# Gate vectors by way of DRAM on GpSimd's queue, and weights, chunks and transposed activations in chosen halves of 128-byte lines

## The chip, the cores and the metric

One Trainium2 chip; the kernel runs on one of its cores. The metric is the device time of one execution in microseconds (us). The run shown is one profiled execution; the times are those of three others.

## What is computed

Two blocks on 256 tokens of width 1024, in float32. The first has two layers with a context of 256 tokens beside x; every layer takes six modulation vectors (shift, scale and gate, twice) from silu(c) times a matrix. The second has four layers of other mixers. Cut to what matters here:

```python
for i in range(2):                                   # first block
    m_lat = silu(c) @ ada_w[i] + ada_b[i]            # for x; m_ctx from c_ctx for the context y
    sh1, sc1, g1, sh2, sc2, g2 = split(m_lat, 6)
    h, hc = rms(x, norm1_g[i]) * (1 + sc1) + sh1, rms(y, norm1_g[i]) * (1 + csc1) + csh1
    o, oc = mixer(h, hc)                             # layer 0: Fourier and window attention; layer 1: neighbourhood
    x = x + g1 * o
    x = x + g2 * swiglu(rms(x, norm2_g[i]) * (1 + sc2) + sh2)
    if i == 0:                                       # the same for the context, with cg1 and cg2
        y = y + cg1 * oc
        y = y + cg2 * swiglu(rms(y, norm2_g[i]) * (1 + csc2) + csh2)
for i in range(4):                                   # second block: retention, convolution, dilated attention, retention
    x = x + rms(mixer(rms(x, w[i, 0])), w[i, 1])
    x = x + rms(swiglu(rms(x, w[i, 2])), w[i, 3])
```

## The kernel before

A product in float32 is made of three fast passes: each operand is split into a high and a low part (`whi` and `wlo` for weights, `hTh` and `hTl` for transposed activations, `ckh` and `ckl` for chunks), and `mm3` (line 484) adds high x high, high x low and low x high. In the profile a matmul stands as out<-moving,stationary.

Weights come in blocks of 1 MB (128 partitions x 2048 float32) on SyncE's queue into one of three raw tiles (`Weights.load`, line 246). ScalarE makes the high part and VectorE the low part, by halves (`Weights.split`, line 280), into a slot: "0" to "2" always, "3" and "4" in some stages. Slot "3" is the place of the context's transposed activations, the second half (e = 1) of the tiles `hTh` and `hTl`; slot "4" is a pool of its own behind the fixed pools.

A first product takes 48 matmuls of 256 columns a block: `mm_nat` (line 495) with hT as weights of TensorE and the block streaming, `mm_trans` (line 504) the other way round. A second product, `mm_down` (line 515), takes 24 matmuls of 512 columns a block, 12 for each of two token tiles, with a chunk (the transposed result of the first product) as weights of TensorE and the block streaming; its accumulators are called acc. In the FFN of layer 0 x and the context share a pass: `FfnPair.emit` streams x's hT and the context's hT, 2 x 256 columns, in one matmul. In the even mixer and in the convolution hT itself is reused to hold the chunks.

`Kernel.open` (line 330) makes the pools in this order, one behind the other in every partition: const (consts, small, half), raw (three raw tiles of 8192 bytes), hl (the slots "0" to "2", six tiles of 8192), x (`hTh` and `hTl`, 16,384 bytes each, then x's two tiles), st (small statistics, 1344 bytes), s4, nb. A tile takes a multiple of 32 bytes, and the first one starts on a 128-byte line. Behind nb each stage opens its own pools, slot "4" and the chunks among them; the pools h1 and ada grow from the other end. Retention's pools start with tiles of which one is 32 bytes long, Odd's with one of 256 and one of 32.

The modulation's rows are added up in a tile `rows` of 128 partitions x 512, one for each layer and group g (`ada_unit`, line 2093): output 512 j + n of x stands in partition 32 j, of the context in 32 j + 1. There are eight units k for each group; they run between other work, those of layer 1 within layer 0's FFN and layer 1's mixer. `gate` (line 2139) spreads one gate vector over all partitions: two DMAs on ScalarE's queue, each from one partition of `rows` into half of the tile `gate`, which takes the place of a tile in nb. It is called six times: twice at the end of the even mixer, twice in the middle of layer 0's FFN (after block 5), once in Odd after the second group of heads, once in layer 1's FFN. `gated` (line 2150) multiplies the accumulators by it and adds them to x.

Each engine runs its instructions in the order in which they are written down, and a DMA that it issues stands in that order too. `Pace` estimates when each engine comes to what has been written so far, DMAs counted; put-off stages and splits of weights are placed by it. GpSimd (POOL) computes the powers `ny` of the norms and adds masks to Odd's biases; its queue loads the norm gains of the second block (`gain`, line 389).

Of the kernel before, what the change touches and what calls it, by code (L numbers as in the profile page):

```python
# [7 lines left out]
F32 = mybir.dt.float32  # L8
# [6 lines left out]
D = 1024  # L15
# [9 lines left out]
HOLD = 1200                # no split where a stage is due within this time ...  # L25
HOLD_AHEAD = 1             # ... unless fewer blocks than this are split ahead

# columns of the packed small inputs
# [9 lines left out]
# columns of the packed constants  # L38
CP = {}
_o = 0  # L40
for _n, _w in (("ident", 128), ("rev", 128), ("sel", 256), ("e2", 8), ("diag", 32)):
    CP[_n] = (_o, _w)
    _o += _w
# [3 lines left out]
HALVES = slice(0, 512), slice(512, 1024)  # L47


class Engine:  # L50
    """Passes an engine's instructions on and keeps the pace's account of them."""
# [14 lines left out]
class Pace:  # L66
    """An estimate of when each engine comes to the instructions emitted so far, from the waits that
    the data needs and the price of each instruction. It only steers the order of emission."""

    LAG = {"pe": 190, "act": 40, "dve": 190, "pool": 190}       # from an engine's end to another's start  # L70
    OWN = {"pe": 0, "act": 190, "dve": 125, "pool": 125}        # ... to its own next instruction
# [12 lines left out]
    def entry(self, ap):  # L84
        """Times of the last write, of its engine, and of the last use, by element of the tile."""
# [25 lines left out]
    def ready(self, *aps):  # L111
        """When the data of these is there for another engine."""
        return max(float(self.view(x, self.entry(x)[0]).max()) + self.LAG.get(self.entry(x)[2], 0) for x in aps)

    def free(self, tag, bufs, n):
        """When the next n tiles of this tag are free."""
        hist = next((v for k, v in self.tags.items() if k and k.startswith(tag)), [])
        return max([float(self.tiles[x][1].max()) for x in hist[-bufs:][:n]], default=0.0) if len(hist) >= bufs else 0.0

    def loaded(self, tile):  # L120
        """A block of weights goes into this tile."""
# [45 lines left out]
    def clock(self, start, end):  # L167
        """The tensor engine runs at half its clock after a window in which it was mostly idle."""
# [36 lines left out]
class Weights:  # L205
    """Streams weight blocks: DRAM -> raw -> (high part, low part), ahead of their use.

    Blocks are split, by halves, where the pace has them landed and the engines that split them idle,
    so that no engine waits on a transfer with other work behind it."""

    def __init__(self, K):
# [4 lines left out]
        self.at = -1             # the last block asked for  # L216
        self.part = None         # the block of which one half is split
# [4 lines left out]
        self.slots = []          # free slots, the longest free first  # L222
# [11 lines left out]
    def close_slot(self, name):  # L234
        """No block goes into this slot any more."""
# [43 lines left out]
    def split(self, u):  # L279
        """The next half of block u."""  # L280
# [45 lines left out]
class Kernel:  # L326
# [3 lines left out]
    def open(self, ex):  # L330
# [10 lines left out]
        self.hT = [self.x_p.tile([128, 2, KD, 256], F32R, name=n) for n in ("hTh", "hTl")]  # L341
        self.W = Weights(self)
        self.tasks, self.attns, self.tagged = [], [], {}
        self.mm_n, self.held = 0, []         # tiles "mm" taken so far; those that put-off stages read: [number, task]
# [3 lines left out]
        self.half = self.const_p.tile([128, 8], F32, name="half")  # L348
        self.nc.gpsimd.memset(self.half, -0.5)
        self.nc.scalar.dma_start(out=self.small, in_=self.a["small"])  # L350
        self.nc.scalar.dma_start(out=self.consts, in_=self.a["c_pack"])

# [4 lines left out]
    def open_ext(self, n):  # L357
        """Room for one more weight block ahead; "3" is the place of the context's h^T."""
# [25 lines left out]
    def post(self, gain, bias=None):  # L384
        """x += rms(acc (+ bias)) * gain, in stages."""
# [31 lines left out]
    def block2(self, bin_):  # L417
        """bin_: the boundary before the first sublayer, its A of both tiles done."""
# [10 lines left out]
    def table(self, func):  # L429
        """Have the scalar engine fetch this function's table ahead of its use."""  # L430
# [13 lines left out]
    def rsqrt(self, ss, n, scale, eps, pool, tag="n", bufs=None):  # L444
        """1/sqrt(ss * scale + eps)."""
# [6 lines left out]
    def square(self, ss, src, b):  # L452
        """ss[:, b] = sum of the squares / D of src, half b of [tok, D]."""
# [4 lines left out]
    def rstd(self, ss):  # L458
        """1/sqrt(ss[:, 0] + ss[:, 1] + eps)."""
# [9 lines left out]
    def split_psum(self, hi, lo, ps, act=True):  # L469
        """hi + lo = ps exactly, each with the bits one fast pass carries."""  # L470
# [4 lines left out]
    def bcast_row(self, row, n):  # L475
        """DMA source: a DRAM row of n elements for every partition."""
        return bass.AP(row.tensor, row.offset, [[0, 128], [1, n]])

# [7 lines left out]
    def mm32(self, out, lhsT, rhs, start, stop, share=1, **k):  # L486
        """A float32 product; share: how many run side by side."""
# [7 lines left out]
    def mm_nat(self, key, hT, t, out, parity=False):  # L495
        """out[tok, 256] = h[tok tile t, or the tokens of parity t] @ w block (K = 1024)."""
# [7 lines left out]
    def mm_trans(self, key, hT, out, need=1):  # L504
        """out[feat, j, tok] = (h @ w block)^T for its two 128-feature tiles."""
# [26 lines left out]
    def room(self, tag, n):  # L532
        """Run put-off tasks of this tag until fewer than n are left."""
# [6 lines left out]
    def defer(self, f, src, need=1, tag=None):  # L540
        """Run f (which takes `need` PSUM tiles) once the tensor engine has come to where src is there."""
# [7 lines left out]
    def stage(self, f, src, eng, tag=None, after=None):  # L549
        """Emit f, work of the engine eng, once that engine need not wait for src and `after` holds."""  # L550
# [1819 lines left out]
```

## Time and profile before

| | us |
|---|---|
| median of three runs | 2721.39 |
| lowest and highest | 2714.77, 2721.40 |
| profiled execution: its span, first to last instruction | 2716.9 |

The profiled execution has no time of its own beside its span; the median of the runs lies 4.5 us above that span. The page gives busy times of the engines, the chain of work that ended last, groups of instructions and the DMA issues. A busy time of TensorE (PE) counts overlapping matmuls once; how fast they follow each other is read from their starts in the timeline. PEclk is the granted clock as a share of full speed.

### The profile page before, as it was taken

To read this page: it belongs to the slowest core of one execution; us is meant where nothing else is said; L and a number is where in the kernel's file an instruction comes from. 1 tells how busy PE (TensorE), PEld (TensorE's weight loads), DVE (VectorE), ACT (ScalarE), POOL (GpSimd) and SP (SyncE) were. 2 spreads that over 40 slices of the span, in tenths; PEclk is the share of its full clock that TensorE was granted. 3 is DMA by queue.
4 is the path that set the end of the run, shared out by engine and by line. 5 is a ranking of instruction groups with operands and counts; after the bars stand their busy time and mean duration, and the time that the engine had idled before them with its cause. 6 is when DMAs were issued, how large, how long until landed. Compare 5 with 4: busy or idle time off the path is not lost.

```text
span 2716.9 us, 43849 instructions
## 1 busy us (share of the span) xinstructions
PE 2599.4 (96%) x18444; PEld 2308.7 (85%) x18444; DVE 1496.4 (55%) x2420; ACT 1202.4 (44%) x2050; POOL 108.5 (4%) x156
## 2 busy tenths in 40 slices
PE   6988997999989999999999979999999999999998
PEld 5646875788867999999999869989998999999997
DVE  4475332346647745765645555456555654765643
ACT  4454221235535544544544434445554544544532
POOL 1100000000311000000000000000000000000000
PEclk9998998999989999999999999999999999999999
DMA  7368257545464675564655736545443654564652
GB/s 259 123 215 153 102 185 125 189 155 184 119 129 137 202 176 181 181 199 142 206 182 168 226 89 212 192 140 175 136 132 118 210 186 155 181 202 140 205 186 82
DMA packets 321414, 453.68 MB, mean 167 GB/s; under 512 B 20689, under 2 KB 280913, under 8 KB 316097
## 3 DMA queue, kind: packets, MB, share of 16 engines
q1 hardware_dynamic: 315552, 434.63, 48.1%
q10 hardware_dynamic: 2592, 5.33, 3.7%
q0 software_dynamic: 3072, 10.91, 1.1%
q8 instruction: 145, 2.38, 0.4%
q14 instruction: 53, 0.43, 0.0%
HBM read 445.47 MB, written 2.23 MB: 165 GB/s over the span
## 4 chain that ended last, share of the span: by engine, by line
PE 83%; DVE 6%; DMA 6%; ACT 2%; issue 1%; ACTq 0%; POOL 0%; SPq 0%; DVEq 0%; POOLq 0%
PE mm L60 62%; PE acc L60 21%; DVE wlo L60 2%; DMA wraw<-ev_w_out 1%; DMA wraw<-ada_w 1%; DMA wraw<-ffn_w_up 1%; DVE sm L60 1%; DVE hTl L60 1%; ACT whi L60 1%; DMA u<-up 1%; DMA wraw<-ffn_w_down 1%; ACTq L60 0%; DMA taps<-u 0%; POOL ny L60 0%; DVE hn L60 0%
## 5 line engine op out<-in xcount | busy, mean ns | idle before, releaser
L60 DVE TENSOR_TENSOR wlo<-wraw,whi 128x1024 fp32r<-128x1024 f32 x592 | 701.3, 1225 | 454.4 <-ACT whi L60 453.5
L60 ACT CAST whi<-wraw 128x1024 fp32r<-128x1024 f32 x592 | 592.4, 1048 | 392.7 <-issue 155.7
L60 PE MATMUL mm<-hTh,whi 128*128 128x256 f32 (+1 forms) x1840 | 553.5, 301 | 17.0 <-ACT whi L60 15.2
L60 PE MATMUL mm<-hTh,wlo 128*128 128x256 f32 (+1 forms) x1840 | 552.0, 300 | 0.6 <-DVE wlo L60 0.5
L60 PE MATMUL mm<-hTl,whi 128*128 128x256 f32 (+1 forms) x1840 | 551.9, 300 | 0.3 <-DVE hTl L60 0.3
L60 PE MATMUL mm<-whi,hTh 128*128 128x256 f32 x1616 | 467.8, 290 | 4.1 <-ACT hTh L60 3.2
L60 PE MATMUL mm<-whi,hTl 128*128 128x256 f32 x1616 | 458.7, 284 | 5.5 <-DVE hTl L60 5.5
L60 PE MATMUL mm<-wlo,hTh 128*128 128x256 f32 x1616 | 457.9, 283 | 0.0
L60 PEld LDWEIGHTS mm<-hTh,whi 128*128 128x128 f32 x1840 | 352.7, 192 | 32.0 <-ACT whi L60 16.0
L60 PEld LDWEIGHTS mm<-hTl,whi 128*128 128x128 f32 x1840 | 351.7, 191 | 13.5 <-DVE hTl L60 0.5
L60 PEld LDWEIGHTS mm<-hTh,wlo 128*128 128x128 f32 x1840 | 351.6, 191 | 13.0 <-DVE wlo L60 1.7
L60 PEld LDWEIGHTS mm<-whi,hTh 128*128 128x128 f32 x1616 | 310.4, 192 | 22.7 <-issue 9.7
L60 PEld LDWEIGHTS mm<-whi,hTl 128*128 128x128 f32 x1616 | 310.4, 192 | 7.6 <-DVE hTl L60 7.6
L60 PEld LDWEIGHTS mm<-wlo,hTh 128*128 128x128 f32 x1616 | 310.9, 192 | 0.6
L60 PE MATMUL acc<-whi,ckh 128*128 128x512 f32 x664 | 264.7, 399 | 0.0
L60 PE MATMUL acc<-whi,ckl 128*128 128x512 f32 x664 | 262.6, 395 | 0.6 <-DVE ckl L60 0.6
L60 PE MATMUL acc<-wlo,ckh 128*128 128x512 f32 x664 | 262.6, 395 | 0.4 <-DVE wlo L60 0.4
L60 PE MATMUL mm<-hTh 128*128 128x256 f32 x656 | 188.3, 287 | 0.5 <-ACT hTh L60 0.5
L60 PE MATMUL mm<-hTh,hTl 128*128 128x256 f32 x656 | 186.7, 285 | 0.4 <-DVE hTl L60 0.4
L60 PE MATMUL mm<-hTl,hTh 128*128 128x256 f32 x656 | 186.4, 284 | 0.0
L60 DVE TENSOR_TENSOR hTl<-wraw,hTh 128x1024 fp32r<-128x1024 f32 x116 | 138.9, 1223 | 59.0 <-ACT hTh L60 58.9
L60 DVE TENSOR_TENSOR sg<-sg,mm 128x512 f32<-128x512 f32 (+1 forms) x67 | 40.2, 600 | 228.2 <-PE mm L60 228.2
(245 smaller groups left out, 3335.2 us busy)
## 6 DMA issues: line engine op xcount, KB each, us to landing
wraw<-ffn_w_in SPq DMA_DIRECT2D x88, 1024.0 KB, 5.1
wraw<-ret_w_in SPq DMA_DIRECT2D x48, 1024.0 KB, 5.2
wraw<-ffn_w_out SPq DMA_DIRECT2D x44, 1024.0 KB, 4.9
wraw<-ada_w SPq DMA_DIRECT2D x40, 1024.0 KB, 5.2
wraw<-attn_w_in SPq DMA_DIRECT2D x36, 1024.0 KB, 5.0
wraw<-ffn_w_down SPq DMA_DIRECT2D x33, 1024.0 KB, 4.9
wraw<-ffn_w_gate SPq DMA_DIRECT2D x22, 1024.0 KB, 5.2
wraw<-ffn_w_up SPq DMA_DIRECT2D x22, 1024.0 KB, 5.3
```

What stands on the lines that cost most here:

```text
L60: r = f(*args, **kw)
```

## The change

Three things. The constants lose two tables that nothing reads (sel, e2; 264 columns). Pads and a stride of 64 bytes within `hTh` and `hTl` move tiles: x's hT starts a 128-byte line, the context's hT and slot "3" start at its middle, and everything behind the pool x moves by 704 bytes, in Retention and Odd by 96 less. And `gate` no longer reads `rows` itself: when a group g > 0 is complete, `save_rows` writes the four rows of x (in layer 0 of the context too) to DRAM, and `gate` reads 1024 elements from there for every partition, in one DMA; both are on GpSimd's queue. The two pads of 96 bytes below are Retention's and Odd's. The rest of the diff takes out comments and the entries of the two tables.

```diff
-for _n, _w in (("ident", 128), ("rev", 128), ("sel", 256), ("e2", 8), ("diag", 32)):
+for _n, _w in (("ident", 128), ("rev", 128), ("diag", 32)):
...
+HT_E = KD * 256 + 16
...
-        self.hT = [self.x_p.tile([128, 2, KD, 256], F32R, name=n) for n in ("hTh", "hTl")]
+        self.pad(self.x_p, 64)
+        self.hT = [self.x_p.tile([128, 2 * HT_E], F32R, name=n).rearrange("p (e c) -> p e c", e=2)[:, :, 0:KD * 256]
+                   .rearrange("p e (k c) -> p e k c", k=KD) for n in ("hTh", "hTl")]
...
+        self.pad(self.const_p, 32)
...
+    @staticmethod
+    def pad(pool, n, name="pad"):
+        pool.tile([128, n // 4], F32, name=name)
...
         K.ck_p = pool("ck", 4)
+        K.pad(p1, 96)
...
         K.ck_p = pool("ck", 2)
+        K.pad(p1, 96)
...
         nc.vector.tensor_tensor(out=t, in0=t, in1=ps, op=ALU.add)
+        if k == KD - 1 and g:
+            self.save_rows(l, g)
...
     def gate(self, l, n, e):
         nc = self.nc
         g, x = (1, 0) if n == "g1" else (2, 1)
-        rows = self.rows[l, g]
+        src = self.saved[l, g, e]
         t = self.nb_p.tile([128, D], F32, tag=("gpost", "gpre")[e], name="gate")
-        for h in range(2):
-            r = 32 * (2 * x + h) + e
-            nc.scalar.dma_start(out=t[:, h * 512:h * 512 + 512], in_=rows[r:r + 1, :].rearrange("p (a n) -> p a n", a=1).to_broadcast([1, 128, 512]))
+        nc.gpsimd.dma_start(out=t, in_=self.bcast_row(src[2 * x:2 * x + 2, :], D))
...
+    def save_rows(self, l, g):
+        for e in range(1 if l else 2):
+            self.saved[l, g, e] = d = self.rows_p.tile([4, 512], F32, name=f"rows{l}{g}{e}")
+            self.nc.gpsimd.dma_start(out=d, in_=self.rows[l, g][e:e + 97:32, :])
...
+        K.rows_p = ex.enter_context(tc.tile_pool(name="saved", bufs=1, space=bass.MemoryType.DRAM))
```

## Rows read from the trace of the kernel before

**Rows 1.** The page: busy times by engine, and the chain's shares by engine.
```profile
PE 2599.4 (96%) x18444; PEld 2308.7 (85%) x18444; DVE 1496.4 (55%) x2420; ACT 1202.4 (44%) x2050; POOL 108.5 (4%) x156
...
PE 83%; DVE 6%; DMA 6%; ACT 2%; issue 1%; ACTq 0%; POOL 0%; SPq 0%; DVEq 0%; POOLq 0%
```

**Rows 2.** Stretches: length, busy us (instructions) by engine, granted clock, DMA share, GB/s.
```profile
900.00:1110.00 210.00, 207.74 (x1486) 195.08 (x1487) 120.28 (x136) 98.49 (x133) 3.68 (x6) 1.00 0.67 199
1110.00:1300.00 190.00, 190.00 (x1341) 177.99 (x1341) 120.09 (x168) 93.42 (x145) 5.49 (x10) 1.00 0.48 160
```

**Rows 3.** Timeline of TensorE: start, duration, instruction; the first matmuls of runs.
```profile
944.41 0.28 PE L60 MATMUL mm<-hTh,whi 128*128 128x256 f32 x1
...
950.06 0.40 PE L60 MATMUL acc<-hTh,ckh 128*128 128x512 f32 x1
...
972.77 0.28 PE L60 MATMUL mm<-hTh,whi 128*128 128x256 f32 x1
...
978.21 0.28 PE L60 MATMUL mm<-hTh 128*128 128x256 f32 x1
...
983.97 0.40 PE L60 MATMUL acc<-whi,ckh 128*128 128x512 f32 x1
...
989.58 0.28 PE L60 MATMUL mm<-hTh,whi 128*128 128x256 f32 x1
...
1001.07 0.39 PE L60 MATMUL acc<-whi,ckh 128*128 128x512 f32 x1
...
1006.55 0.28 PE L60 MATMUL mm<-hTh 128*128 128x256 f32 x1
```

**Rows 4.** DMA issues: out<-in, queue, count, KB each, median us to landing.
```profile
gpre<-norm_w POOLq DMA_DIRECT2D x8, 512.0 KB, 5.7
...
gate<-rows ACTq DMA_DIRECT2D x12, 256.0 KB, 21.4
```

**Rows 5.** Stretches while gates are in flight; columns as in group 2.
```profile
222.00:236.00 14.00, 14.00 (x66) 11.65 (x65) 11.24 (x19) 6.11 (x12) 0.57 (x1) 0.99 0.91 34
...
985.00:1010.00 25.00, 25.00 (x170) 23.12 (x169) 9.16 (x9) 7.70 (x9) 0.00 (x0) 1.00 0.93 107
```

**Rows 6.** The chain of waits in order of time: start, length, what.
```profile
203.95 12.45 ACTq L60
...
219.96 22.15 DMA wraw<-ev_w_out
...
404.32 21.79 PE mm L60 x96
...
430.42 20.94 DMA wraw<-ffn_w_up
...
483.29 23.44 PE mm L60 x110
...
512.52 23.63 PE mm L60 x112
```

**Rows 7.** Groups of matmuls by form: count, busy us, mean ns, idle before.
```profile
L60 PE MATMUL mm<-whi,hTh 128*128 128x256 f32 x1616 | 467.8, 290 | 4.1 <-ACT hTh L60 3.2 <-ACT qT L60 0.8
...
L60 PE MATMUL acc<-whi,ckh 128*128 128x512 f32 x664 | 264.7, 399 | 0.0
...
L60 PE MATMUL mm<-hTh,whi 128*128 128x512 f32 x288 | 113.5, 394 | 15.2 <-ACT whi L60 15.2
```

**Rows 8.** Timeline of GpSimd around the first and third gates; idle before in brackets.
```profile
226.03 0.57 POOL L60 TENSOR_TENSOR ny<-nv,half 128x1 f32<-128x1 f32 x1 [118.22 <-DVE nv L60]
...
779.36 1.80 POOL L60 TENSOR_TENSOR bias<-bias,mask 128x768 f32<-128x768 f32 x1 [14.08 <-DMA bias<-od_rel_bias]
```

**Rows 9.** One stretch, TensorE alone: length, busy us (matmuls), clock, DMA share, GB/s.
```profile
199.00:262.10 63.10, 51.07 (x213) 0.86 0.86 152
```

**Rows 10.** Timeline of TensorE in layer 1's mixer; idle before in brackets.
```profile
774.33 0.28 PE L60 MATMUL mm<-whi,hTl 128*128 128x256 f32 x1
786.33 1.94 PE L60 MATMUL mm<-consts,sm 128*128 128x128 f32 x8 [11.73 <-DVE sm L60]
```

More of the change, by code (lines that the diff above doesn't have):

```diff
@@ L2159, in gated @@
         return update
-    for f in (ada_plan, ada_unit, mods, cols, gate, gated):
+    for f in (ada_plan, ada_unit, mods, cols, gate, save_rows, gated):
         setattr(Kernel, f.__name__, f)
@@ L2175, in build @@
             K.W.open_slot(K.slot(K.hl_p), str(i))
-        K.rows, K.mod, K.gates = {}, {}, {}
+        K.rows, K.saved, K.mod, K.gates = {}, {}, {}, {}
+        K.rows_p = ex.enter_context(tc.tile_pool(name="saved", bufs=1, space=bass.MemoryType.DRAM))
         ada1 = [(1, g, k) for g in range(3) for k in range(KD)]
@@ L2258, in constants @@
         pk[b * 64:b * 64 + 64, o + b * 64:o + b * 64 + 64] = np.eye(64)[::-1]
-    o = CP["sel"][0]
-    for j in range(4):
-        for e in range(2):
-            pk[32 * j + e, o + 128 * e:o + 128 * e + 128] = 1
-    o = CP["e2"][0]
-    for j in range(4):
-        for e in range(2):
-            pk[32 * j + e, o + 2 * j + e] = 1
     o = CP["diag"][0]
```

## The prediction

> **What bounds the kernel now.** I read the busy times and the chain of waits first. TensorE is busy for 96% of the span, and 83% of the chain that ended last runs through it [rows 1]; from 900 us on its busy time nearly equals each stretch [rows 2]. So two things count: how far apart matmuls start, and the few places where TensorE stands still. "Busy" overlaps from one matmul to the next, so I took starts instead.
>
> The starts show a pattern in the addresses. I worked out where each tile lies from the order and sizes of the pools. Before, consts, small and half take 2208 + 2560 + 32 = 4800 bytes of a partition, 37 lines of 128 bytes and a half, so raw blocks, the weight slots "0" to "2" and hTh/hTl (all multiples of 128) start in odd halves. The small tiles of the pool st add 1344 bytes, ten lines and a half, so the stage pools behind it, with most chunks and slot "4", start in even halves (in Retention and Odd 32 bytes further). A matmul streams one operand while the next one's weights are loaded, so I sorted starts by whether both operands start in the same half.
> - 256 columns, same half: from 978.21 to 983.97 there are 48 matmuls, 120.0 ns each. Over all such runs of ten or more the mean is 119.8.
> - 256 columns, opposite halves (slot "4" against hT): 944.41 to 950.06, 48 matmuls, 117.7 ns; 972.77 to 978.21, 48 matmuls, 113.3 ns. A run holds one value or the other: 27 runs near 117.8, 14 near 113.4, mean 116.4.
> - 512 columns, opposite halves (chunks against slots): 983.97 to 989.58, 24 matmuls, 233.8 ns; mean 233.4.
> - 512 columns, same half: 1001.07 to 1006.55, 24 matmuls, 228.3 ns; 227 in other runs [all rows 3].
>
> So the two widths want opposite things. All this is at a granted clock of 1.00, the level of 2.4 GHz [rows 2].
>
> Next, the stalls. A gate's half takes 21.4 us to land, for 256 KB; a row of norm_w, 512 KB from DRAM to all partitions on the GpSimd queue, takes 5.7 [rows 4]. While the gates are in flight the DMA engines are about nine tenths busy, and 34 GB/s move [rows 5]. Weight blocks queue behind them: the chain waits 22.15 us for one of ev_w_out, and 20.94 us for one of ffn_w_up in the first FFN [rows 6].
>
> **The change, part by part.**
>
> *Addresses, 256 columns.* After, the constants take 1152 + 2560 + 32 + 32 = 3776 bytes (29 lines and a half), so weights stay odd; 64 more bytes put x's hT in even halves, and the 64 bytes inside put the context's hT, which is also slot "3", in odd ones. Everything behind moves by 704 bytes, so even becomes odd; 96 bytes make up for the odd-sized tiles of Retention and Odd. The program has 11,520 such matmuls (three groups like the first of [rows 7] are 4,848 of them). 33 blocks of 48 (1,584) use slot "4" and lie opposite already. 17 blocks of the context (816) stay in the same half. The other 9,120 go from same to opposite: 9,120 x (119.8 - 116.4 ns) = 31.0 us. Bounds by the two values a run can hold: 9,120 x 2.0 = 18 and 9,120 x 6.4 = 58 us. I take the mean, as nothing in the rows tells what picks the value.
>
> *Addresses, 512 columns.* 88 blocks of 24 second products (2,112; most are the three groups like the second of [rows 7]) go from opposite to same: 2,112 x (233.4 - 228.3) = 10.8 us; bounds 10 and 14. Seven blocks (168), where hT itself holds the chunks (the even mixer for x, the convolution), go the other way: -0.9. In the FFN of x and context, 3 x 288 matmuls stream x's half and then the context's (the last of [rows 7]): half of each stream becomes opposite. No row shows that; bounds 0 and 864 x 6.5 ns = 5.6 us of loss, and I take the middle, -2.8. Sum: 38.1 us.
>
> What of this reaches the end: of the 9,120, all but 1,008 lie after 900 us, where TensorE is busy 207.74 of 210.00 and 190.00 of 190.00 us [rows 2]. I count 95%, 36 us; bounds 20 (all runs at 117.8, full loss in the pair) and 69.
>
> The Trainium skill speaks against this part. Its page "SBUF — State Buffer", section "SBUF: two separate sides", says that among the engines only the port pair of VectorE and GpSimd is contended, and that TensorE never waits on anyone. By that rule no address matters and this part is worth nothing; the rows show starts that differ by 6 ns between runs at the same clock, and the rows decide.
>
> *Gates.* Removed: twelve DMAs on ScalarE's queue, each reading one partition 128 times over. Added: six DMAs on GpSimd's queue that write four rows of 2 KB to DRAM when a group of modulations is complete, and six that read 4 KB per partition, like norm_w's. GpSimd waits for the sum of the rows and for the write to land; behind that stand only its small powers and the bias additions. Around the first gates it is idle for 118 us until 226.03 [rows 8], and the gates are first needed at the end of the first token tile, 72 matmuls x 0.228 = 16 us after the products begin: more than 5.7. So I cost the added work at nothing; without that cover it would be one landing, about 6 us.
> - First pair, layer 0's mixer: from 199.00 to 262.10 TensorE runs 213 matmuls, 192 of them second products [rows 9], worth 192 x 0.228 + 2 = 46 us. 17 us are lost; ScalarE alone sat 12.45 us on an issue [rows 6]. I take 16.
> - Second pair: the FFN's rhythm is 29.4 us a step (29.23 from 483.29 to 512.52, plus the two matmuls that the first piece lacks). From 404.32 to 483.29 two steps took 79.0 instead of 58.9 [rows 6]. Of these 20 us the new transfers may use 1 to 5; I take 17.
> - Layer 1's first gate: TensorE stands from 774.33 to 786.33 for a softmax [rows 10], whose mask addition on GpSimd waited 14.08 us for a bias transfer [rows 8] issued behind the gate. I take 11 of 12.
> - Layer 1's second: no stall, TensorE 25.00 of 25.00 us although DMA is at 0.93 [rows 5]. Nothing.
>
> Sum 44 us; bounds 30 (a boundary stays late in the first pair, the scores in the third) and 50. What is late next in these places is TensorE itself.
>
> *The constants.* 264 columns less to load at the start: ahead of work that waits for the first modulation blocks anyway; nothing, bounds 0 and 1 us. The order of emission may shift by a few us either way, since the planner counts these DMAs; that is inside the bounds.
>
> **Sum.** Span 2716.9 - 36 - 44 = 2637. The runs' median lies 4.5 us above the profiled span, so 2641.
>
> **Rivals.**
> 1. *The halves don't matter.* The difference in [rows 3] would then come from something else about slot "4", as its place after the pools. Then only the gates gain: 2721.4 - 44 = 2677; the Trainium skill's page named above leads here too. Against it: chunks against slots "0" to "2" show the difference with the other sign, and slot "3" (same half as hT) shows 120.0 like the ordinary slots. 7%.
> 2. *The gates' stalls are replaced.* Other transfers hold the blocks up: 2721.4 - 36 = 2685. Against it: norm_w's rows land in 5.7 us with no stall beside them. 5%.
> 3. *Slower: opposite halves cost more for 256 columns.* With 512 columns opposite halves cost 5 ns more than the same half. If the order in which x's hT (now even) meets odd weights falls into that phase, 256 columns could take over 120 ns too. The gates' 44 us and the 10 us of 512 columns are used up from 54/9,120 = 5.9 ns on, at 125.7 ns; at 127 ns the time is 2721.4 - 54 + 66 = 2733. Against it: neither order of moving and stationary operand shows more than 118 in slot "4". 3%.
> 4. *All runs lock at 113.* 2721.4 - 69 - 44 = 2608. 10%; it lies in my forecast's own range.
>
> **How the numbers follow.** The forecast, with rival 4, has 85%; its bounds are 2721.4 - 20 - 30 = 2671 and 2721.4 - 69 - 50 = 2602. The range reaches from 2606 to 2678, to take in rival 1. A measurement of this kernel tells about 0.3% (8 us) from no change. Faster by more: 85 + 7 + 5 = 97, less 1 for mixtures: 96%. Same 1%, slower 3%.
>
> **What would show it.** Runs of 256-column matmuls against x's hT start 113 to 118 ns apart, the context's still 120; second products 227 to 229. The gates land in about 6 us; no piece of ScalarE's queue above 2 us on the chain; steps of 29 us through both gates of the FFN, with the granted clock at 1.00 there. Wrong would be: 120 ns with x's hT, a wait for gate rows on GpSimd ahead of a boundary, or new waits for weight blocks in the FFNs.

## The result, and the profile after

| | us |
|---|---|
| after, median of 4 runs | 2652.99 (2651.98 to 2653.34) |
| before, median of 4 runs | 2721.39 (2714.77 to 2722.09) |
| ratio, with its 95% interval | 0.9758 (0.9744 to 0.9772) |
| after, profiled execution: time and span | 2652.94, 2651.2 |

The change takes 68 us off, 2.4%. The forecast was 2641 with a range of 2606 to 2678: the sign and the range held, the middle was 12 us too low. The page first, busy times and the chain's shares:

```profile
PE 2566.9 (97%) x18444; PEld 2278.8 (86%) x18444; DVE 1494.3 (56%) x2420; ACT 1202.5 (45%) x2050; POOL 116.7 (4%) x168
...
PE 86%; DVE 6%; DMA 3%; ACT 3%; issue 1%; SPq 1%; POOL 1%; POOLq 0%; DVEq 0%; ACTq 0%
```

Against [rows 1], DMA on the chain falls from 6% to 3%, and TensorE is busy for 32.5 us less with the same number of matmuls. The piece of 12.45 us on ScalarE's queue [rows 6] is gone from the chain. Both parts of the change have left their mark: fewer waits, and matmuls that follow each other faster.

The gates in the DMA issues (queue, count, KB each, median us to landing), and their neighbours on GpSimd's timeline in layer 1's mixer:

```profile
gpre<-norm_w POOLq DMA_DIRECT2D x8, 512.0 KB, 5.6
...
gate<-rows POOLq DMA_DIRECT2D x6, 512.0 KB, 5.7
...
rows<-rows POOLq DMA_DIRECT2D x6, 8.0 KB, 4.8
```

```profile
706.38 0.60 POOL L61 DMA_DIRECT2D gate<-rows  x1
...
736.74 1.81 POOL L61 TENSOR_TENSOR bias<-bias,mask 128x768 f32<-128x768 f32 x1 [3.73 <-DVE qn L61]
```

A whole gate lands as fast as a row of norm_w, 5.7 us instead of 21.4 for each half [rows 4]. In the second of these views the addition of the mask no longer waits for a bias transfer, as it did for 14.08 us [rows 8]; TensorE's 11.73 us for the softmax [rows 10] is gone with it.

The same stages on the chain (start, length, what), and TensorE from the first second products to the end of the even mixer (length, busy us, granted clock, DMA share, GB/s):

```profile
200.58 22.26 PE acc L61 x96
...
223.71 11.20 PE acc L61 x48
...
235.79 11.19 PE acc L61 x48
...
383.63 5.78 PE acc L61 x24
389.41 23.85 PE mm L61 x112
413.26 5.78 PE acc L61 x24
```

```profile
199.00:246.00 47.00, 47.00 (x221) 1.00 0.62 218
```

The 192 second products run through in 46 us, as the prediction counted for them without stalls, where [rows 9] had 51 busy us in 63 at a clock of 0.86. In layer 0's FFN the step from one group of second products to the next is 413.26 - 383.63 = 29.63 us, also across the place where [rows 6] had waits of 21 us. In the stage from 199 to 246 us TensorE is busy all the time, at a granted clock of 1.00, the level of 2.4 GHz.

Now the starts of runs in layer 1's FFN and in Retention, TensorE's timeline as in [rows 3]:

```profile
935.17 0.28 PE L61 MATMUL mm<-hTh 128*128 128x256 f32 x1
...
940.96 0.40 PE L61 MATMUL acc<-whi,ckh 128*128 128x512 f32 x1
...
946.56 0.28 PE L61 MATMUL mm<-hTh,whi 128*128 128x256 f32 x1
...
952.21 0.28 PE L61 MATMUL mm<-hTh,whi 128*128 128x256 f32 x1
...
957.86 0.39 PE L61 MATMUL acc<-whi,ckh 128*128 128x512 f32 x1
...
963.32 0.28 PE L61 MATMUL mm<-hTh 128*128 128x256 f32 x1
...
1054.19 0.28 PE L61 MATMUL mm<-whi,hTh 128*128 128x256 f32 x1
...
1056.91 0.28 PE L61 MATMUL mm<-whi,hTh 128*128 128x256 f32 x1
```

- 256 columns, x's hT against ordinary slots: 946.56 to 952.21, 48 matmuls, 117.7 ns; with the weights streaming, 1054.19 to 1056.91, 24 matmuls, 113.3. Forecast: 113 to 118. Right.
- 256 columns with slot "3": 935.17 to 940.96, 48 matmuls, 120.6 ns, although slot "3" now lies opposite to x's hT. Forecast 116.4 on average. Wrong.
- 512 columns, chunks against slots "0" to "2", now in the same half: 940.96 to 946.56, 24 matmuls, 233.3 ns, what [rows 3] had for opposite halves. Forecast 228. Wrong.
- 512 columns with slot "4": 957.86 to 963.32, 24 matmuls, 227.5 ns. Right.

The third of these is the step that failed; the second is a smaller miss of its own. In the means over all runs of a trace: 256 columns went from 119.32 to 117.01 ns (11,327 pairs of matmuls: 26.2 us), 512 columns from 232.48 to 231.49 (2,722 pairs: 2.7 us), and the matmuls that stream x's and the context's hT from 226.85 to 229.14 (857 pairs: 2.0 us lost). The experiments ask first what each part is worth, then what it is in the addresses that counts, then what it is about the gates.

### The profile page after: what moved, and what is told of

Read it like the earlier page. It is cut to its first block, busy times and chain, and to the rows that moved or that the text cites. A ratio compares the mean times of both kernels' runs of the same rounds, so it can differ in the third digit from the quotient of the medians.

```text
span 2651.2 us, 43863 instructions
## 1 busy us (share of the span) xinstructions
PE 2566.9 (97%) x18444; PEld 2278.8 (86%) x18444; DVE 1494.3 (56%) x2420; ACT 1202.5 (45%) x2050; POOL 116.7 (4%) x168
## 4 chain that ended last, share of the span: by engine, by line
PE 86%; DVE 6%; DMA 3%; ACT 3%; issue 1%; SPq 1%; POOL 1%; POOLq 0%; DVEq 0%; ACTq 0%
PE mm L61 62%; PE acc L61 24%; DVE wlo L61 2%; DMA wraw<-ada_w 1%; DVE hTl L61 1%; DVE sm L61 1%; DMA u<-up 1%; ACT whi L61 1%; POOL ny L61 1%; DMA taps<-u 1%; DMA wraw<-od_w_in 0%; ACT sm L61 0%; DVE hn L61 0%; ACT hTh L61 0%; SPq L1977 0%
## 5 line engine op out<-in xcount | busy, mean ns | idle before, releaser
L61 PE MATMUL mm<-whi,hTh 128*128 128x256 f32 x1616 | 462.2, 286 | 4.6 <-ACT hTh L61 3.2
L61 PE MATMUL mm<-whi,hTl 128*128 128x256 f32 x1616 | 452.7, 280 | 5.6 <-DVE hTl L61 5.6
L61 PE MATMUL mm<-wlo,hTh 128*128 128x256 f32 x1616 | 452.0, 280 | 0.0
L61 PEld LDWEIGHTS mm<-hTh,whi 128*128 128x128 f32 x1840 | 346.5, 188 | 17.3 <-ACT hTh L61 2.0
```

Of the source, the lines that this page charges most:

```text
L61: r = f(*args, **kw)
```

## The experiments

"Place" is an address mod 256, worked out from the order and the sizes of the pools as the prediction did it. After the change, weights in slots "0" to "2" have place 64, most chunks and slot "4" 192, x's hTh 128 and hTl 0, the context's hTh 192 and hTl 64. Times are medians, each compared with runs of the kernel before on the same chip.

### The gates alone

Before's code and addresses, with `save_rows` and the new `gate`.

> The kernel before with the gate vectors by way of DRAM on the GpSimd queue; every tile stays at its address. Theory: the two parts of the change act in different places and add up. The stages that hold the gates gained about 40 us in the trace of after (start of the layer-0 mixer's second products to the end of layer 1's mixer: 43 us, less what addresses give there), so 2721.4 - 40 = 2681 us (2673 to 2690); the gates land 4 to 8 us after their issue, 256-column starts stay at 119.8 ns and 512-column ones at 233.4. Rival: part of those 40 us was the faster matmuls, which the weight stream followed; then the gates alone are worth 30 or less, 2691 or more.

Measured: 2676.3 us, ratio 0.9839 (0.9822 to 0.9855): 43.5 us less than before. The starts are before's, 119.8 and 233.4 ns. The gates are worth what the prediction said (44), and a little more than I had read off the trace of after. By place, from the starts of second products in the two traces: 15.5 us in the even mixer (forecast 16), 22 in layer 0's FFN (17), 10 in layer 1's mixer (11); 4.3 us are lost ahead of the even mixer's second products and 2 around the start of layer 1's FFN. The first of these need not be the gates: that stretch is 2.6 us longer than before's in the trace with the addresses alone, and 1.2 us shorter in the one that reads every gate twice in the same order. No run here explains the second.

### The addresses alone

After's code with before's `gate` and without `save_rows`.

> The kernel after, with the gates as before (twelve broadcasts out of one SBUF partition each, on ScalarE's queue); only the addresses differ from the kernel before. Theory: the addresses are worth what the trace of after shows by starts, 9,120 x (119.8 - 116.9) = 26.5 us at 256 columns and 2,112 x (233.4 - 231.45) = 4 us at 512, less 2 us in the FFN of x and context, of which 95% reach the end: 27, so 2694 us (2688 to 2700). The forecast's own terms would give 2685. Rival: the broadcasts' stalls swallow part of the faster matmuls ahead of layer 1 (they wait for weights anyway), then 2700 to 2705.

Measured: 2700.2 us, ratio 0.9930 (0.9915 to 0.9944): 19.6 us. Up to 860 us the trace gains nothing (1.6 us late), from there 17 us. So the forecast's 36 is out, and 27 as well; the time lies where the rival's range begins. Beside the gates the same addresses are worth 2676.3 - 2653.0 = 23.3 us, and all of that comes after 817 us in the traces too. Parts of the chain of this kernel, and the gates among the DMA issues:

```profile
205.50 13.09 ACTq L61
...
222.15 22.60 DMA wraw<-ev_w_out
...
430.93 20.93 DMA wraw<-ffn_w_up
...
455.40 17.21 DMA wraw<-ffn_w_down
```

```profile
gate<-rows ACTq DMA_DIRECT2D x12, 256.0 KB, 21.4
```

The stalls of [rows 6] are back to within a microsecond. That they swallow the faster matmuls, as the rival has it, is not shown: ahead of layer 1's FFN the addresses gain next to nothing beside the gates either, where these stalls are gone. Only 1,008 of the 9,120 matmuls of 256 columns stand ahead of 900 us, and the FFN of x and context, which stands there too, loses 2.0 us. The two parts' own gains, 43.5 and 19.6, add to 63 of the 66 to 68 of both.

### 128 bytes more ahead of the stage pools

No half changes, but chunks and slot "4" go from place 192 to 64, where the weights lie.

```diff
+        self.pad(self.x_p, 128, "pad2")
         self.W = Weights(self)
```

> The kernel after with 128 more bytes between h^T and the stage pools: every half of a 128-byte line stays what it is, but most chunks and slot 4 go from 192 to 64 mod 256, where slots 0 to 2 lie. Theory A (512 columns want equal places mod 256, and 128 bytes apart is nearly as bad as opposite halves): 1,388 more second products start as the equal ones of after do, 228.8 instead of 232.5 ns, 5.1 us, and slot 4's 256-column ones go from 118.3 and 117.3 to 117.7 and 114.5, 1 to 2 us: 2646 us (2644 to 2649). Theory B (only the half counts, as the prediction had it; what keeps 512 columns at 231.5 is something else, such as the phase that the run before leaves): 2653 us and starts at 231.5 as in after.

Measured: 2643.7 us, ratio 0.9724 (0.9710 to 0.9739), whose interval lies wholly below that of after: this kernel beats before and after, and comes out just below theory A's range. Two runs of second products in its timeline, the one with a slot "0" to "2", the other with slot "4":

```profile
935.58 0.39 PE L61 MATMUL acc<-whi,ckh 128*128 128x512 f32 x1
...
941.07 0.28 PE L61 MATMUL mm<-hTh,whi 128*128 128x256 f32 x1
...
952.30 0.40 PE L61 MATMUL acc<-whi,ckh 128*128 128x512 f32 x1
...
957.78 0.28 PE L61 MATMUL mm<-hTh 128*128 128x256 f32 x1
```

24 matmuls take 5.49 us, 228.8 ns each, where after took 233.3 for the same run. Over all runs, 512 columns at equal places start 228.0 ns apart (1,758 pairs), those still 128 bytes apart 232.5 (412 pairs); the mean falls from 231.49 to 229.16. Within a run the first nine matmuls or so vary from 224 to 236, and then each takes 226 or 227. Theory B, the halves of the prediction, has fallen for 512 columns: what its rows of "the same half" had in common was the same place mod 256.

### 64 bytes more ahead of the stage pools

As before, with a pad of 64 instead of 128: chunks and slot "4" go to place 0, opposite to the weights.

> The kernel after with 64 more bytes between h^T and the stage pools: chunks and slot 4 return to even halves, as in the kernel before, while x's h^T stays even. So the 512-column products are opposite again and the 256-column ones with slot 4 lie in the same half. By halves alone: 1,949 second products return to 233.4 ns (+2 us against after's 232.3) and 1,560 products of slot 4 to 119.8 (+3 us): 2658 us (2656 to 2661). By places mod 256: 56 second products of after with weights at 64 and chunks at 0 started 229.3 ns apart although opposite; if that holds for the 1,592 that lie so here, they gain 5 us, and slot 4 costs up to 3: 2648 to 2652.

Measured: 2652.5 us, ratio 0.9754 (0.9739 to 0.9768): the same as after, not the 2658 of the halves and half a microsecond above the range of the places. Second products with the weights at 64 and chunks at 0 start 229.3 ns apart (1,567 pairs), 3 ns faster than after's in the same half. Slot "4" costs back most of what they gain: the mean over 256 columns rises from 117.01 to 117.28. Again the half is not what counts for 512 columns.

### Products alone, at all pairs of places

> Not the kernel: it leaves the whole computation out and only starts TensorE products, with no other engine at work, 48 at a time of 256 columns (operands taken as the first products take theirs) and of 512 (as the second products), with moving and stationary tiles at all pairs of offsets in steps of 32 bytes mod 256; then the 16 pairs in steps of 64 bytes again in another order. Theory A (the start-to-start time is set by the places of the two operands mod 256, through TensorE's own reads): 512 columns 228 to 229 ns at equal places, 229 to 230 with the moving operand 64 bytes on, 232 to 233 at 128 or 192; 256 columns 120 at 64 against 64, 114 to 116 with the moving one at 64 and the stationary one at 128, 117 to 118 the other way round; the second pass gives the same. Theory B (the places matter only because other engines read and write the same lines meanwhile): one value for each width at all offsets, near the lowest of the kernel, 113 and 226. Theory C (a run's value is a phase left by what came before): the second pass differs from the first by as much as the offsets do.

Measured: 1403.8 us, in a single run. Its timeline at four pairs, moving operand at place 128, stationary at 128, 192, 0 and 64; in each, 48 matmuls of 256 columns from the first row and 48 of 512 columns from the second:

```profile
55.42 0.28 PE L51 MATMUL acc<-mvh,sth 128*128 128x256 f32 x1
...
61.18 0.40 PE L51 MATMUL acc<-mvh,sth 128*128 128x512 f32 x1
...
72.09 0.28 PE L51 MATMUL acc<-mvh,sth 128*128 128x256 f32 x1
...
88.97 0.28 PE L51 MATMUL acc<-mvh,sth 128*128 128x256 f32 x1
...
94.41 0.39 PE L51 MATMUL acc<-mvh,sth 128*128 128x512 f32 x1
...
105.60 0.28 PE L51 MATMUL acc<-mvh,sth 128*128 128x256 f32 x1
...
122.48 0.28 PE L51 MATMUL acc<-mvh,sth 128*128 128x256 f32 x1
...
128.17 0.40 PE L51 MATMUL acc<-mvh,sth 128*128 128x512 f32 x1
...
139.37 0.28 PE L51 MATMUL acc<-mvh,sth 128*128 128x256 f32 x1
...
156.33 0.28 PE L51 MATMUL acc<-mvh,sth 128*128 128x256 f32 x1
...
161.99 0.40 PE L51 MATMUL acc<-mvh,sth 128*128 128x512 f32 x1
...
172.98 0.28 PE L51 MATMUL acc<-mvh,sth 128*128 128x256 f32 x1
```

So 120.0 and 227.3 ns at equal places, 113.3 and 233.1 with the stationary operand 64 further, 118.5 and 233.3 at 128, 117.9 and 229.0 at 192. Over all 64 pairs the time goes with the difference of the two places, to about 1 ns, but for one pair at difference 192 that held 113.3 ns and not 117.8. The means of both passes:

| stationary less moving place, mod 256 | 0 | 32 | 64 | 96 | 128 | 160 | 192 | 224 |
|---|---|---|---|---|---|---|---|---|
| 256 columns, ns | 119.9 | 118.3 | 113.8 | 117.3 | 118.6 | 120.0 | 117.4 | 117.5 |
| 512 columns, ns | 227.0 | 233.3 | 233.3 | 234.3 | 232.9 | 233.4 | 229.0 | 233.3 |

Theory A holds, B falls: no other engine is at work here, so the places of TensorE's own two operands are enough for these times. Of C a part remains: the second pass repeats the first to about 1 ns but for 256 columns at difference 64 (three of four pairs at 113 to 114, one at 117.8, where the first pass had 113.3). Summed over the pairs of each trace, the table gives 2176.8 us for the products of before and 2138.4 for those of after; the means of the traces give 2178.5 and 2151.8. The 13 us that after is short of the table are at 256 columns, about half of them where both operands come from hT, which is where slot "3" is at work, and the rest where hT streams against the other slots. For 512 columns the table carries over to the kernels; for 256 it does so only in part.

### hTh and hTl at the same place

The 128 bytes of the faster kernel moved between the two tiles; both at 128, chunks still at 64.

```diff
-        self.hT = [self.x_p.tile([128, 2 * HT_E], F32R, name=n).rearrange("p (e c) -> p e c", e=2)[:, :, 0:KD * 256]
-                   .rearrange("p e (k c) -> p e k c", k=KD) for n in ("hTh", "hTl")]
-        self.pad(self.x_p, 128, "pad2")
+        self.hT = []
+        for n in ("hTh", "hTl"):
+            t = self.x_p.tile([128, 2 * HT_E], F32R, name=n).rearrange("p (e c) -> p e c", e=2)[:, :, 0:KD * 256]
+            self.hT.append(t.rearrange("p e (k c) -> p e k c", k=KD))
+            if (128, 0)[len(self.hT) - 1]:
+                self.pad(self.x_p, (128, 0)[len(self.hT) - 1], "pad" + n)
```

> The kernel with 128 more bytes ahead of the stage pools (2643.7 us), but these bytes now stand between hTh and hTl, so that x's two parts of h^T both lie at 128 mod 256 (hTl lay at 0), the context's at 192; chunks stay at 64, weights at 64. By the table that the kernel with products alone gave (start to start by the stationary operand's place less the moving one's, mod 256): products that stream h^T (difference 192) 117.4 to 118 ns throughout, those that stream weights (difference 64) 113.8 to 114.3, the 857 of the FFN of x and context 227.6 instead of 229.1. Sum over all products 0.6 us less: 2643 us (2641 to 2645). Rival: where high and low parts lie at different places, each run pays for the alternation (256 columns measured 116.8 in the kernel with 128 more bytes, against 115.9 from the table); then one place for both gives up to 0.9 x 11.3 thousand = 10 us: 2633.

Measured: 2647.5 us, ratio 0.9735 (0.9721 to 0.9750), above the range. Products that stream hT against weights take 117.55 ns, as expected; those that stream weights 115.7, not 114. The FFN of x and context missed altogether: 233.4 ns instead of 227.6, 857 x 4.3 = 3.7 us, about the 3.8 by which the kernel is slower; the other changes cancel. At the same difference of the first half, 192, the trace has 227.3 where hTl lies elsewhere and 233.4 where both lie alike; the table, read by the first half, does not carry over to streams of two pieces, and no run here says why. (Where both parts of hT lie alike, the time is near what the table has for the worse of the two pieces: 232.9 for 128 here, 233.3 for 64 in the next kernel.)

The rival hoped for 10 us from unmixed places. The mean over 256 columns stays at 116.88, but two opposite changes hide in it. Products that stream x's hT against slot "3", where both operands had their high and low parts at different places, fall from 120.6 to 115.5 ns over 991 pairs, 5 us (with the slot streaming they stay at 117.8). One run of them, 48 matmuls at 113.3 ns up to the next row:

```profile
931.89 0.28 PE L61 MATMUL mm<-hTh 128*128 128x256 f32 x1
...
937.33 0.39 PE L61 MATMUL acc<-whi,ckh 128*128 128x512 f32 x1
```

Products that stream weights from the other slots lose as much, 114.3 to 115.7 ns over 3,829 pairs. So the rival holds for slot "3", where the mixed places kept the kernel after at 120.6 ns, and has fallen for the program as a whole.

### Both at place 0

As the kernel above, with 192 bytes ahead of hTh instead of 64, and 128 behind hTl.

> As the kernel before this one, but x's two parts of h^T both lie at 0 mod 256, weights and chunks at 64, the context's h^T at 64. By the table: the sign turns round, products that stream h^T (5,405, difference 64) 113.8 ns, those that stream weights (4,919, difference 192) 117.4; the FFN of x and context 232 to 233 where the first half of a stream decides; sum over all products 1.6 us more than with h^T at 128: 2645 us (2642 to 2648). Rival (a moving operand in an odd half with the stationary one in an even half is the fast case, as in every kernel so far): products that stream h^T stay at 117.7, those that stream weights at 115: 2646 us, told apart by the starts, not by the time.

Measured: 2648.6 us, ratio 0.9736 (0.9720 to 0.9753), just above the range. Products that stream weights at difference 192 take 117.46 ns, as the table has it and not 115, so the rival (a moving operand in an odd half is fast) has fallen. Those that stream hT at difference 64 take 116.8 on average: a fifth at 113 or 114, the others near 118. The 113 of the table is there, but most runs do not settle on it. Slot "3" takes 117.3 ns here, again less than 120.6. What picks one of the two values at difference 64 stays open.

### All places 64

The gates alone, with 192 bytes between hT and the stage pools, so that weights, hT, chunks and slot "4" all have place 64.

> The gates by way of DRAM, and every operand of the products at 64 mod 256: weights and h^T as in the kernel before, and 192 bytes ahead of the stage pools for chunks and slot 4. Against the kernel with the gates alone (2676.3 us): the 512-column products go from 232.4 to 228 ns (2,722 x 4.1 = 11 us gained, less where Retention's and Conv's chunks stand 32 bytes further), slot 4's 256-column ones from 116.4 to 119.9 (1,553 x 3.5 = 5 us lost), so by the table 2673 us, by the prediction's terms 2671. If 512 columns stay near 231.5 although all places are equal, neither the halves nor the table are right: 2681.

Measured: 2669.9 us, ratio 0.9816 (0.9800 to 0.9832), 6.4 us less than the gates alone. 256 columns take 119.84 ns, 10,048 of 10,911 pairs exactly 120; 512 columns 227.67 where places are equal (2,171 pairs) and 233.2 where the chunk stands 32 bytes further (412 pairs). This is the cleanest view that the two widths want opposite things, and it confirms the price of 512 columns that the prediction had, under its right condition.

### The gates from DRAM on ScalarE's queue

```diff
-        nc.gpsimd.dma_start(out=t, in_=self.bcast_row(src[2 * x:2 * x + 2, :], D))
+        nc.scalar.dma_start(out=t, in_=self.bcast_row(src[2 * x:2 * x + 2, :], D))
```

> The kernel after, but the gate vectors are read from DRAM on ScalarE's queue instead of GpSimd's. Theory S (the source was the trouble: one partition read 128 times over): they land in 4 to 8 us as in after, ScalarE sits on an issue for at most 2 us plus the wait for the rows; 2653 us (2650 to 2660). Theory Q (the queue was the trouble, ScalarE's work standing behind its own DMA issues): 12 us pieces on ScalarE's queue return, 2665 to 2690.

Measured: 2651.6 us, ratio 0.9757 (0.9742 to 0.9771), the same as after. The DMA issues have:

```profile
gate<-rows ACTq DMA_DIRECT2D x6, 512.0 KB, 4.7
```

The queue does not matter once the source is DRAM, and nor does the time of the reading: the second pair is read at 410 us here and at 264 us in after.

### The gates from one partition on GpSimd's queue

Against the addresses alone, above:

```diff
-            nc.scalar.dma_start(out=t[:, h * 512:h * 512 + 512], in_=rows[r:r + 1, :].rearrange("p (a n) -> p a n", a=1).to_broadcast([1, 128, 512]))
+            nc.gpsimd.dma_start(out=t[:, h * 512:h * 512 + 512], in_=rows[r:r + 1, :].rearrange("p (a n) -> p a n", a=1).to_broadcast([1, 128, 512]))
```

> The kernel after, but the gate vectors are read as before, out of one partition of the rows in SBUF, and on GpSimd's queue; nothing is written to DRAM. Theory S (source): the halves still take some 20 us to land at 34 GB/s and weight blocks still wait behind them; the kernel with the gates as before took 2700 us, of which at most the 12.45 us that ScalarE sat on an issue come back: 2688 to 2700. Theory Q (queue): 2653 to 2662.

Measured: 2726.4 us, ratio 1.0028 (1.0016 to 1.0039): 0.3% slower than before, although the faster addresses are in it. The source is the trouble, as theory S has it (one partition in pieces of 2 KB for each partition against DRAM in one of 4 KB; the size of the pieces was not varied by itself); but S's time missed, since I gave back ScalarE's wait and thought of no new one. On the chain:

```profile
203.06 38.62 DMA wraw<-ev_w_out
...
299.63 28.74 DMA wraw<-ffn_w_gate
...
920.82 21.93 DMA wraw<-ffn_w_up
```

The four broadcasts of the first pair are now issued within 1.6 us (199.55 to 201.14) and land at 211.84, 222.60, 232.42 and 241.20, one after the other, some 10 us for 256 KB; the weight block behind them lands at 241.69. On ScalarE's queue the four of before landed no sooner (210.71, 220.63, 231.23 and 239.59), so the 38.62 us are mostly the old stall under another name: up to the end of the even mixer this trace loses 5.6 us against the addresses alone. The largest loss, 14.5 us, is in layer 1's FFN. There GpSimd's queue reads the gate at 918.65 us, where ScalarE's queue had come to it at 984.80 without a stall, and a weight block waits 21.93 us behind it.

### Every gate read twice

```diff
-        nc.gpsimd.dma_start(out=t, in_=self.bcast_row(src[2 * x:2 * x + 2, :], D))
+        for _ in range(2):
+            nc.gpsimd.dma_start(out=t, in_=self.bcast_row(src[2 * x:2 * x + 2, :], D))
```

> The kernel after, with every gate vector read from DRAM twice over into its tile, one transfer behind the other on GpSimd's queue. If the new transfers lie wholly beside other work, as the forecast counted them, the time stays: 2653 us (2651 to 2655). If a gate's landing is on the path to a boundary or holds weight blocks up, each doubled gate costs its 4 to 8 us: up to 6 gates, 2660 to 2690.

Measured: 2660.3 us, ratio 0.9785 (0.9769 to 0.9801), 7.3 us more than after. That speaks against gates at no cost, but by the starts of the same matmuls in both traces 5.9 of its 8.1 us come after 1417 us, where no gate is in flight; another 3.9 in layer 0's FFN stand at one split of weights at 440 us, long after the gates had landed (280 us), and 1.7 are gained elsewhere. The planner counts DMAs, so the order of work had shifted: on VectorE the low part of one block now stands behind other work, just where the 3.9 us are lost, and on TensorE one group of transposes of `un` stands elsewhere, at 1542 us. The later loss is mostly the clock. Two stretches of this kernel's trace (length, busy us and matmuls of TensorE, granted clock, DMA share, GB/s):

```profile
1458.00:1462.60 4.60, 4.58 (x28) 0.69 0.67 261
...
1774.10:1781.70 7.60, 7.60 (x52) 0.78 0.58 196
```

The same work in the trace of after:

```profile
1455.80:1459.10 3.30, 3.29 (x28) 1.00 0.95 356
...
1767.60:1773.60 6.00, 6.00 (x53) 1.00 0.46 146
```

With a third such place, at 1587 us, that is 4 of the 5.9 us at a clock that lies in part at the lower level, 1.2 GHz. TensorE waits for other engines ahead of these places in both kernels, so the rows do not tell why only one of them lost its clock. The next kernel takes the shifted order away.

### Every gate read twice, in the same order

```diff
-        nc.gpsimd.dma_start(out=t, in_=self.bcast_row(src[2 * x:2 * x + 2, :], D))
+        for pool in nc.gpsimd, self.tc.nc.gpsimd:
+            pool.dma_start(out=t, in_=self.bcast_row(src[2 * x:2 * x + 2, :], D))
```

> As the kernel with every gate vector read twice, but the second read is not told to the planner, so that the order of work on TensorE is that of the kernel after to the last instruction. The kernel with gates read twice took 2660.3 us instead of 2653; of its 8.1 us in the trace 6.6 came up after 1417 us, where no gate is in flight, and 3.7 in the FFN of x and context (1.3 and 1.2 us were gained elsewhere). If those come from the shifted order, this kernel takes 2653 us (2651 to 2655); if the second transfers hold something up, 2658 to 2662.

Measured: 2652.8 us, ratio 0.9759 (0.9746 to 0.9773), after's time. Its DMA issues:

```profile
gate<-rows POOLq DMA_DIRECT2D x12, 512.0 KB, 5.2
```

Its order of work on TensorE, ScalarE, VectorE and GpSimd is that of after to the last instruction. Twice the reads, no more time: the new reads lie wholly beside other work. The six writes to DRAM were not doubled; that they cost nothing is only implied by the gates' 43.5 us. The kernel ahead of this one is 7 us slower with the same reads, but how much of that is the order is not settled: 3.9 us stand where the order changed, and a lower clock comes and goes at the same order too. This kernel's trace has, where after had 1.00:

```profile
1764.00:1771.60 7.60, 7.60 (x52) 0.78 0.60 200
```

## Why the prediction was right, and which of its steps were not

- **What bounds the kernel.** Right: TensorE's starts and a few stalls. Each of the two parts alone is faster than before, by 43.5 and 19.6 us.
- **Gates, 44 us.** Right: 43.5 alone. The split was off by up to 5 us: in layer 0's FFN the prediction kept back 1 to 5 us for the new transfers and took 17; they landed by 271 us, ahead of the FFN's first second products at 324, and the place gave 22. Small losses elsewhere made up for it, which is luck in the sum. The 21.4 us that it read as the time of a half hold the wait for the halves ahead of it: they land some 10 us apart. And the 34 GB/s are those of the first of the two stretches in [rows 5]; the second moved 107.
- **The added work at nothing.** Shown for the reads, by doubling them in the same order; not shown by itself for the writes. "The order of emission may shift by a few us" was right too: with six more DMAs that the planner counts, 3.9 us were lost where the order had changed.
- **256 columns, 31.0 us.** The sign is right, the size somewhat less: 26.2 us by the means of the starts, 116.9 ns instead of 116.4 for the products in opposite halves. For this width the halves sort the table rightly (119.9 and 118.6 ns at differences 0 and 128, 113.8 and 117.4 at 64 and 192), but they are not the condition: the same two halves give 113.8 or 117.4 by which operand lies 64 further. Slot "3" (120.6) did not gain because hTh and hTl, unlike before, lay at different places; with both alike it took 115.5. What picks 113 or 118 at difference 64 was unknown to the prediction and is still open.
- **512 columns, 10.8 us.** This is the step that failed: "88 blocks go from opposite to same", priced by rows of 228 ns. It gave 2.7 us, together with the seven blocks that go the other way, where 9.9 were forecast for both. The rows of [rows 3] with 228 had both operands in the same half, but also at the same place mod 256, chunks at 128 against slot "4" at 128. After, chunks are at 192 and weights at 64: the same half, 128 bytes apart, 232.5 ns. I read the coarser of two conditions that the rows could not tell apart. With 128 bytes more, 512 columns fall to 229.16 ns, worth 6.3 us of the 9.3 by which the kernel falls to 2643.7. That this is near the 2641 forecast for the change as it stood does not bear the forecast out: its 256 columns and its share to the end were too high as well.
- **The FFN of x and context, -2.8 us.** Measured -2.0, inside the bounds.
- **95% to the end, 36 us.** The sum by the measured means is 26.2 + 2.7 - 2.0 = 26.9; 23.3 reached the end beside the gates, 19.6 without them. None of it came ahead of layer 1's FFN, where few of these matmuls stand.
- **The span.** Forecast 2637, measured 2651.2: 13 us are the addresses (36 against 23.3), and 1 or 2 the gates. That the median lies 4.5 us above the span held for before's pair of numbers only; here 1.7 us lie between the profiled time and its span, so 2.8 us of the error cancelled, by luck.
- **The rivals.** "The halves don't matter" was right in its first word and wrong in its time: places matter, and by more than one bit. The Trainium skill, "SBUF — State Buffer", section "SBUF: two separate sides", says that TensorE never waits on anyone; the products alone do not speak against that, as their starts differ from 113 to 120 ns with every other engine idle. What does not follow is that addresses are free: the difference lies between TensorE's own two operands. "All runs lock at 113" did not happen: between x's hT and slots "0" to "2" the mean is 114.4 ns where the weights stream, and 117.6 where hT does.

## What to carry to other kernels

Before using a pattern in addresses, list every condition that the fast rows share, not only the one that you looked for, and measure the bare operation over all offsets: one run of products alone would have priced 512 columns rightly, and 256 columns only in part. A broadcast out of one partition is slow at its source; write the row to DRAM and read it from there, on any queue. When a planner counts what you add, compare with a kernel whose order is the same, and compare the granted clock of the stretches that differ, or a shift of the order or of the clock passes for a cost.

## What the runs showed of the hardware

- The time from one fast float32 product to the next depends on the stationary operand's address less the moving one's, mod 256 bytes: 113.3 to 120.0 ns for 256 columns, 227.0 to 234.3 for 512, with TensorE alone at work and a granted clock of 1.00. Equal places are best for 512 columns and nearly worst for 256.
- At a difference of 64, runs of 256 columns hold 113 or 118 ns; products alone mostly hold the first, the kernel with hT at place 0 mostly the second. At 192, 11 of 12 runs of products alone hold 117.8 and one 113.3.
- Where x's hT streams against slot "3" and both have their high and low parts at different places (128 and 0 against 192 and 64, kernel after), 256 columns take 120.6 ns; with both parts alike, at difference 64, 115.5 in one kernel and 117.3 in another.
- Streams of two pieces do not follow the table by their first piece: 226.7 ns with everything at 64, 233.4 with both parts of hT at 128 or at 0, 227.3 and 232.6 in turn where one lies at 128 and the other at 0.
- For the gap of single, isolated matmuls the Trainium skill, "TensorE: Matmul & The Clock Gate", section "Back-to-back issue gap", gives N / 2.4 + 2.5 ns. By this formula an estimate for the two widths is 109 and 216 ns. Here every product loads a stationary operand, and no run of products came below 113.3 and 226 on average.
- Four broadcasts of 256 KB, each out of one partition, land about 10 us apart, and a weight block queued behind them waited 38.62 us; the same gates read from DRAM, 512 KB at a time, land in 4.7 to 5.7 us.
